# Attention 0 of a two-layer trunk: rotation stores, strip, key and query loads at other steps, weight pairs one further ahead, the last row's root taken alone

## The chip, the cores and the metric

The kernel runs on one core of a Trainium2 chip. It uses TensorE (PE, matmuls and transposes), VectorE (DVE), ScalarE (ACT), GpSimd (POOL) and SyncE (SP), which issues nearly all DMAs. The metric is the device time of one execution in microseconds. Three runs of the kernel before took 1458.23, 1456.97 and 1454.82 us, median 1456.97; the profiled execution took 1457.22 us.

## The reference

A two-layer encoder trunk on one sequence of 1024 tokens, width 1024, all in f32. Layer 0 is differential attention, layer 1 latent attention (MLA); each has a root-mean-square norm, an adaLN shift, scale and gate from a conditioning vector, a gate path, an output projection and a residual. Cut to layer 0 and the step into layer 1:

```python
h = rmsnorm(x, norm_g) * (1 + scale) + shift          # mod = silu(c) @ ada_w + ada_b
q, k, v, z = split(h @ w_in, 4)                       # 1024 columns each
q, k = rope(q), rope(k)                               # 8 heads x 2 parts x 64
for each head:                                        # v: 128 columns a head
    p0, p1 = softmax(q0 @ k0.T / 8), softmax(q1 @ k1.T / 8)
    o = (p0 - lam * p1) @ v
o = rmsnorm(o, subln_g) * (1 - lambda_init) * silu(z)
x = x + gate * (o @ w_out)
h = rmsnorm(x, norm_g1) * (1 + scale1) + shift1       # input of layer 1
```

## The kernel before, in words

**Precision.** f32 matmuls are made of three reduced ones (`mm3`, lines 178 to 180): each operand is split into a high part (a copy to the reduced format, on ACT) and a low part (a subtraction, on POOL or DVE). For weights that is `split_raw`: `wh` by ACT (L223), `wl` by POOL (L224), from a raw half strip `wraw` or `zraw` in SBUF.

**Stages**, by time of the profiled execution: norm and first projections to about 115 us; from 115 to 170 the z0 products (`z0_pair`), which make keys and queries of heads 2, 4 and 6 with seven products instead of eight and so need weight combinations as well; the value tiles to 245 us, with the first head's scores; attention 0 from 245 to 730; output projection 0 to 800; the norm into layer 1 (`group0`, rows in two groups of four 128-token tiles `xf[0..7]`) to 840; layer-1 projections to 1020; attention 1 to 1380; output projection 1 and the final norm.

**Attention 0** goes head by head. A head has eight steps, one for each tile of 128 queries: score matmuls (L1131) of `ks` against `qa` and `qb` (high and low), softmax on DVE and ACT giving `e`, transposes `tr` (L433), their high and low parts `pth` (ACT) and `ptl` (DVE), and value products `pv` on `vt`. Between these TensorE takes matmuls of `stream0`, the projection of the heads still to come: `gen_strips0` goes through `ORDER0`, the (kind, head) strips of keys, queries and gates. A strip has 16 stream steps `u`, eight for each token half, and two raw half strips; a half strip is split at u = 5 or 13 of the strip before. A head takes 32 stream steps.

**The side queue.** Small jobs wait in `side`; each stream step and each query step calls `tick`, which takes one entry off (None is a tick in which nothing is done). A projected half of keys or queries goes through `rot_job`: `fetch` (DMAs that bring rows swapped by 32 partitions), `first_`, `second` (POOL multiplications and addition), `high` (ACT's copy to the reduced format, `rp_sw`), `low` (POOL's subtraction, `rp_raw`) with the stores of both to DRAM (`hS`, L403). Keys and queries of heads 2, 4 and 6 come from the z0 products earlier; they lie in DRAM (`rS`) and are *parked*: each finished gate half (`z_done`) takes one of them into the side queue.

**Loads of a head.** `bring(h, i)` is called after step i of head h: at i = 0 it loads this head's second query half, at 4 the next head's keys (`load_k`, six DMAs), at 7 the next head's first query half (`load_q`, four DMAs, L838). Values (`vt`, L424) are loaded when a head's first value product is written. The POOL multiplications `ob` prepare output weights; `bc_d`, `bc_s` (L458, L460) broadcast a head's row norms through DRAM.

**What sets the order.** Every engine runs its instructions in a fixed order, SP's DMAs included: a DMA whose data is not ready holds what stands behind it. The order comes from the program above as a scheduling pass arranges it by its own costs; POOL's operations in the attention are held in program order (`in_turn`), ACT's copies behind the last softmax step (`behind`). So a load at another step can also move matmuls on PE.

Of the kernel before, what the change touches and what calls it, by code (L numbers as in the profile page):

```python
# [12 lines left out]
F32R = mybir.dt.float32r  # L13
# [22 lines left out]
    VEC[_n] = (NVEC, _c)  # L36
    NVEC += _c
DEF = 7
ROT = 3
FILL0 = ((1, 1, 1, 1, 1, 0), (1, 0, 1, 0, 1, 0)) * 4  # L40
FILL6 = ((1, 1, 1, 1, 0, 0), (1, 0, 1, 0, 1, 0)) * 2 + ((1, 1, 1, 0, 1, 0), (1, 0, 1, 0, 0, 0)) * 2
FILL1 = ((1, 0, 1, 0), (0, 1, 0, 0)) * 4
# [42 lines left out]
def trunk(ctx: ExitStack, tc: tile.TileContext, A, out):  # L85
# [283 lines left out]
    def rot_job(kind, h, half, eng, raw=None):  # L369

        cs = slice(half * HF, half * HF + HF)
        b = {"raw": raw}
        turn_ = in_turn if eng is G else lambda ins: ins

        def rpt(name):
            return wp.tile([P, HF], F32, name=name, tag="rp", bufs=6)

        def fetch():
            src = b["raw"]
            if src is None:  # L380
                src = rS[kind][h][half]
                b["raw"] = rpt("rp_raw")
                SP.dma_start(b["raw"], src)
            b["sw"] = rpt("rp_sw")
            for q in range(4):
                SP.dma_start(b["sw"][q * 32 : q * 32 + 32], src[(q ^ 1) * 32 : (q ^ 1) * 32 + 32])

        def first_():
            b["r"] = rpt("rp_r")
            turn_(eng.tensor_mul(b["r"], b["raw"], cosT[:, cs]))  # L390

        def second():
            turn_(eng.tensor_mul(b["sw"], b["sw"], sinT[:, cs]))
            turn_(eng.tensor_add(b["r"], b["r"], b["sw"]))

        def high():
            with behind("S"):
                S.copy(b["sw"].bitcast(F32R), b["r"])

        def low():  # L400
            turn_(eng.tensor_sub(b["raw"].bitcast(F32R), b["r"], b["sw"]))
            for l_, t in enumerate((b["sw"], b["raw"])):
                SP.dma_start(hS[kind][h][half][l_], t)  # L403

        return fetch, first_, second, high, low

    def slots(kind, h, half):
        return hS[kind][h][half].rearrange("l (c p) d -> p (l c) d", c=2)
# [404 lines left out]
    def rot_done(kind, h):  # L813
        def f(acc, half):
            raw = wp.tile([P, HF], F32, name="rp_raw", tag="rp", bufs=6)
            if kind:
                S.copy(raw, acc)
            else:
                S.mul(raw, acc, SC0)
            fetch, *steps = rot_job(kind, h, half, G, raw)  # L820
            fetch()
            side.add(*[None] * ROT, *steps[:2], None, *steps[2:])
        return f

    def load_k(h):
# [15 lines left out]
    def z_done(h):  # L841
        def f(acc, half):
            t = wp.tile([P, HF], F32, name="zth", tag="rp", bufs=6)
            S.activation(t, acc, AF.Tanh, scale=0.5)
            V.scalar_tensor_tensor(out=t, in0=t, scalar=1.0, in1=acc, op0=ALU.add, op1=ALU.mult)
            SP.dma_start(zS[h, half], t)
            if parked:
                fetch, *steps = rot_job(*parked.pop(0), G)
                side.add(fetch, None, None, *steps[:2], None, *steps[2:])
        return f  # L850

    def load_gate(h, half):
# [4 lines left out]
    def raw_of(kind, h, f):  # L857
        raw = wst.tile([P, HF], F32, name="wraw", tag="wraw", bufs=2)
        SP.dma_start(raw, A["w_s0"][kind, h, f])
        return raw  # L860

    def gen_strips0(ready, raws):

        w = ready
        for i, (kind, h) in enumerate(ORDER0):
            consume = (z_done if kind == 2 else lambda h: rot_done(kind, h))(h)
            nxt = ([], [])
            u = 0
            for half in range(2):
                for _ in gen_half(w, h0, half, lambda acc: consume(acc, half)):  # L870
                    if i + 1 < len(ORDER0) and u in (5, 13):
                        for a, b in zip(nxt, split_raw(raws.pop(0), 4)):
                            a += b
                    if i + 2 < len(ORDER0) and u in (8, 15):
                        raws.append(raw_of(*ORDER0[i + 2], u > 8))
                    u += 1
                    yield
            w = nxt
# [99 lines left out]
    def z0_weights():  # L978

        for _ in FRONT:  # L980
            a11, a12, a21, a22 = zraw[:4]
            del zraw[:4]
            w = split_raw(a11, 4)
            s1, s4 = zrt("zs1"), zrt("zs4")
            V.tensor_add(s1, a21, a22)
            V.tensor_sub(a21, a11, a21)
            V.tensor_sub(a11, s1, a11)
            V.tensor_sub(s4, a12, a11)
            yield w
            for t in (a12, s4, a11, s1, a21, a22):  # L990
                yield split_raw(t, 4)

    def product0(rhs):

# [78 lines left out]
    for half in range(2):  # L1073
        for _ in gen_half(wz0, h0, half, lambda acc: z_done(0)(acc, half)):
            side.tick()
    zq.append(next(zw))

    def late(p, i):
        if p + 1 < len(FRONT):
# [347 lines left out]
        gate_step0()  # L1427

    def bring(h, i):
        if h and i == 0:  # L1430
            load_q(h, 1)
        if h < NH - 1 and i == 4:
            load_k(h + 1)
        if h < NH - 1 and i == 7:
            load_q(h + 1, 0)

    for h in range(NH - 1):
# [260 lines left out]
    def add0(tt, acc, f, final=False):  # L1698
        V.tensor_add(xf[tt][:, halves[f]], xf[tt][:, halves[f]], acc)
        if final:  # L1700
            SP.dma_start(x1S[tt][:, halves[f]], xf[tt][:, halves[f]])
            junk = p3.tile([P, HF], BF16, name="tjunk", tag="tjunk", bufs=1)
            S.activation(junk, xf[tt][:, halves[f]], AF.Square, accum_out=(ssa, ssb)[f][tt // 4][:, tt % 4 : tt % 4 + 1])

    def group0(gi):
        fulls = [[x_] for x_ in xf[4 * gi : 4 * gi + 4]]
        V.tensor_add(ssa[gi], ssa[gi], ssb[gi])
        norm_x(ssa[gi], fulls, (2, 3) if gi else (1, 2, 3))

        def chunk(k):  # L1710
            if gi == 1:
                h1[k][1] = xt2k("h1h"), xt2k("h1l")
                h1f[k] = ut(f"h1f{k}", dt=F32)
            else:
                h1[k][0] = [h1p.tile([P, HF], F32R, name="h1_" + x_, tag="h1", bufs=16) for x_ in "hl"]
            lm["V"] = h_chunk(1, fulls, k, h1[k][gi], p3x, V, act=not gi and k in (0, 2), f32=h1f[k] if gi else None)
            if gi == 0:
                lm["h"] = h_chunk.act
                if k in (0, 4):
                    lm["h0"] = h_chunk.act  # L1720

        if gi == 0:
            side.add(*[None] * G_WAIT)
        side.add(*[lambda k=k: chunk(k) for k in ((0, 4, 1, 5, 2, 6, 3, 7) if gi else range(KT))])

    def step(sp, i):
        for _ in range((3, 3, 2, 0)[i]):
# [53 lines left out]
    for n, rows, acc, f in ((3, 4, Z, 1), (4, 0, Z, 1), (5, 4, Y, 1), (6, 4, Y, 0)):  # L1781
# [5 lines left out]
        for i in range(4):  # L1787
# [6 lines left out]
                    side.tick()  # L1794
            for j in (i,) if n < 6 or i > 1 else range(2) if i else ():
                add0(rows + j, acc[j], f, n > 3)
            if n == 4:
                SP.dma_start(x1S[i][:, halves[0]], xf[i][:, halves[0]])
                junk = p3.tile([P, HF], BF16, name="tjunk", tag="tjunk", bufs=1)
                S.activation(junk, xf[i][:, halves[0]], AF.Square, accum_out=ssa[0][:, i : i + 1])  # L1800
# [900 lines left out]
```

## Time and profile before

| | us |
|---|---|
| median of three runs | 1456.97 |
| profiled execution, its span | 1457.22, 1455.3 |
| PE, DVE, ACT, POOL busy | 1386.1, 1001.3, 734.0, 709.3 |
| share of the ending chain: PE, DVE, DMA, POOL | 65%, 11%, 7%, 6% |
| z0 products, 115 to 170: PE busy of 55 | 48.62 |
| attention 0, 245 to 730: PE busy of 485 | 445.66 |
| norm into layer 1, 800 to 840: PE busy of 40 | 36.66 |

Rows of the table by stage give the window, then busy time and instructions (x) of PE, its weight loads, DVE, ACT and POOL, then the granted PE clock (1 is full speed), the DMA share and GB/s. Rows of waits give engine and line, what ended the wait, and us in total, times, longest. Rows of the timeline give start, duration, engine, line, operation, output and inputs, and in brackets the idle time before and what ended it. A line is that of the kernel before; lines of the changed kernel stand a little higher.

### The profile page before, as it was taken

The page shows a single profiled execution, that of the slowest core. Times are in us where ns is not written, and L with a number is a line of the kernel's source. Part 1 is how long each engine was busy: PE and PEld are TensorE (multiplying, and loading weights), DVE is VectorE, ACT ScalarE, POOL GpSimd, SP SyncE. Part 2 cuts the span into 40 slices and gives each one's busy share as a digit, 9 for nine tenths or more (in the row PEclk, how much of TensorE's full clock was granted, in tenths as well). Part 3 has the DMA queues.
Part 4 walks back from the last instruction along what each step waited for, and adds up shares of the span by engine and source line. Part 5 has one row for each costly group of instructions (what it writes and reads, how often), then busy time and mean ns, then how long its engine had stood idle before and what let it go on. Part 6 is the DMA issues. An engine that isn't in the chain of part 4 may idle for free.

```text
span 1455.3 us, 20936 instructions
## 1 busy us (share of the span) xinstructions
PE 1386.1 (95%) x7298; PEld 1147.5 (79%) x7298; DVE 1001.3 (69%) x1408; ACT 734.0 (50%) x1331; POOL 709.3 (49%) x553
## 2 busy tenths in 40 slices
PE   9998899899899989999899999999999999999997
PEld 6786687788777767878788788887888888888886
DVE  7699726898678565868869796753655655455584
ACT  5533413555556454656755754334554454445554
POOL 5425730554577563734578423443023174653773
PEclk9999999999999989999999999999999999999999
DMA  9855788677668675676675415669644346565473
GB/s 344 278 163 187 231 219 247 195 217 203 195 194 244 180 222 159 211 197 194 218 245 176 143 52 164 206 216 266 200 117 131 101 124 213 179 229 172 145 269 116
DMA packets 176779, 282.41 MB, mean 194 GB/s; under 512 B 23457, under 2 KB 60449, under 8 KB 176674
## 3 DMA queue, kind: packets, MB, share of 16 engines
q1 hardware_dynamic: 176674, 281.08, 62.5%
q8 instruction: 57, 0.93, 0.3%
q14 instruction: 48, 0.39, 0.1%
HBM read 182.49 MB, written 86.98 MB: 185 GB/s over the span
## 4 chain that ended last, share of the span: by engine, by line
PE 65%; DVE 11%; DMA 7%; POOL 6%; issue 6%; ACT 4%; SPq 1%; POOLq 0%; ACTq 0%; DVEq 0%
PE s L2315 10%; PE tr L433 6%; PE acc L180 5%; PE acc L178 5%; PE acc L179 5%; PE s L1131 4%; PE pv L178 3%; PE pv L179 3%; PE pv L180 3%; PE zacc L180 2%; PE zacc L178 2%; PE zacc L179 2%; DMA qa<-hS 2%; PE vps L178 1%; PE oy L179 1%
## 5 line engine op out<-in xcount | busy, mean ns | idle before, releaser
L436 DVE TENSOR_TENSOR ptl<-tr,pth 128x512 fp32r<-128x512 f32 x256 | 175.9, 687 | 157.1 <-ACT pth L435 151.8
L435 ACT CAST pth<-tr 128x512 fp32r<-128x512 f32 x256 | 150.4, 587 | 254.6 <-PE tr L433 245.7
L450 DVE TENSOR_REDUCE nm<-s 128x1 f32<-128x1024 f32 x192 | 233.1, 1216 | 39.5 <-PE s L1131 30.6
L224 POOL TENSOR_TENSOR wl<-wraw,wh 128x512 fp32r<-128x512 f32 (+2 forms) x65 | 90.5, 1393 | 263.4 <-ACT wh L223 225.9
L452 ACT ACTIVATE e<-s,nm 128x1024 f32<-128x1024 f32 x128 | 143.3, 1120 | 98.4 <-DVE nm L450 92.6
L433 PE MATMUL tr<-ident,e 128*128 128x128 f32 x1024 | 157.5, 276 | 6.6 <-DVE ptl L436 5.9
L433 PEld LDWEIGHTS tr<-ident,e 128*128 128x128 f32 x1024 | 121.0, 142 | 51.4 <-DVE ptl L436 29.5
L178 PE MATMUL pv<-pth,vt 128*128 128x256 f32 x512 | 148.9, 291 | 1.4 <-DMA vt<-vS 1.4
L179 PE MATMUL pv<-ptl,vt 128*128 128x256 f32 x512 | 147.9, 289 | 0.0
L180 PE MATMUL pv<-pth,vt 128*128 128x256 f32 x512 | 145.3, 284 | 0.0
L180 PE MATMUL acc<-h0h,wl 128*128 128x512 f32 x264 | 109.1, 414 | 9.6 <-POOL wl L224 9.6
L178 PE MATMUL acc<-h0h,wh 128*128 128x512 f32 x264 | 109.4, 415 | 4.8 <-ACT wh L223 4.3
L1131 PE MATMUL s<-ks,qa 128*128 128x512 f32 x256 | 89.4, 431 | 21.3 <-DVE e L1139 7.8
L179 PE MATMUL acc<-h0l,wh 128*128 128x512 f32 x264 | 107.0, 405 | 0.0
L178 PEld LDWEIGHTS pv<-pth,vt 128*128 128x128 f32 x512 | 98.4, 192 | 5.4 <-DMA vt<-vS 2.2
L179 PEld LDWEIGHTS pv<-ptl,vt 128*128 128x128 f32 x512 | 98.5, 192 | 2.0
L180 PEld LDWEIGHTS pv<-pth,vt 128*128 128x128 f32 x512 | 98.4, 192 | 0.8
L1475 POOL TENSOR_TENSOR wol<-wol,woh 128x512 fp32r<-128x512 f32 x56 | 82.4, 1493 | 25.5 <-ACT woh L1474 23.8
L1131 PE MATMUL s<-ks,qb 128*128 128x512 f32 x256 | 83.5, 405 | 1.6 <-DMA qb<-hS 1.6
L1139 DVE SCALAR_TENSOR_TENSOR e<-s,z,e 128x1024 f32<-128x1024 f32 x64 | 82.1, 1284 | 2.0
L224 POOL TENSOR_TENSOR wl<-zraw,wh 128x512 fp32r<-128x512 f32 (+2 forms) x36 | 50.7, 1414 | 62.4 <-ACT wh L223 41.7
L452 ACT ACTIVATE s<-s,nm 128x1024 f32<-128x1024 f32 x64 | 70.1, 1095 | 7.1 <-DVE nm L450 6.9
(470 smaller groups left out, 3595.0 us busy)
## 6 DMA issues: line engine op xcount, KB each, us to landing
ada<-in_ada_ss SPq DMA_DIRECT2D x32, 512.0 KB, 5.6
vt<-vS SPq DMA_DIRECT2D x32, 512.0 KB, 5.5
wol<-tS SPq DMA_DIRECT2D x56, 256.0 KB, 5.1
wraw<-in_w_s SPq DMA_DIRECT2D x52, 256.0 KB, 3.2
vS<-v_hl SPq DMA_DIRECT2D x24, 512.0 KB, 5.9
tS<-ob SPq DMA_DIRECT2D x48, 256.0 KB, 3.9
bc_s<-bc_d SPq DMA_DIRECT2D x34, 256.0 KB, 4.0
gz<-zS SPq DMA_DIRECT2D x32, 256.0 KB, 4.2
```

What stands on the lines that cost most here:

```text
L178: PE.matmul(psum, ah, bh, start=first, stop=False, skip_group_check=skip)
L179: PE.matmul(psum, ah, bl, start=False, stop=False, skip_group_check=skip)
L180: mm3.last = PE.matmul(psum, al, bh, start=False, stop=last, skip_group_check=skip).ins
L224: sub = (V if pair_of else G).tensor_sub(l_[:, :n], raw[:, :n], f32v(h_[:, :n]))
L433: transpose_p.last = PE.transpose(tr[:, j, :], p[:, kt * P : (kt + 1) * P], ident).ins
L435: mk["S"] = S.copy(pth[kh][:, :, dst], tr).ins
L436: mk["V"] = V.tensor_sub(ptl[kh][:, :, dst], tr, f32v(pth[kh][:, :, dst])).ins
L450: mk["V"] = V.reduce_max(nm, s_ps, axis=AX.X, negate=True).ins
L452: mk["S"] = S.activation(e, s_ps, AF.Exp, bias=nm, scale=1.0, accum_out=zs).ins
L1131: PE.matmul(s_ps[:, kc * HF : (kc + 1) * HF], src[:, c, ql], KS[h][kc][:, c, :], start=fst, stop=not fst)
L1475: sub = eng.tensor_sub(lo, raw, f32v(hi))
L2315: PE.matmul(s_ps[:, kc * HF : (kc + 1) * HF], lhs, rhs(kc), start=i == 0, stop=i == 4)
```

## The change

1. **Stores.** The store of a rotated tile is a step of its own (`store`), not part of `low`. For stream halves two ticks (ROT) pass ahead of `first_`, not three; `high` and `low` come two ticks sooner, and the store comes two ticks behind `low`, in the tick where it stood before. For parked halves `high` and `low` come one tick sooner, the store one later.
2. **Strip loads.** A raw half strip is loaded at u = 12 (first half) of the strip two before, or u = 3 (second half) of the strip before, not at u = 8 and 15 of the strip two before.
3. **Keys and queries.** `bring` loads the next head's keys at i = 2 (was 4), its first query half at i = 5 or 6 (was 7), and the second half of odd heads at i = 1 (was 0).
4. **Weight pairs.** Two pairs of z0 weights are split ahead of the first product (was one), so `product0` runs two ahead; every fourth pair goes into buffers of the tag `gz`, which the gates of heads use later (`split_z`).
5. **Last row.** In `group0(1)` the sum and root of rows 4 to 6 are taken as soon as row 6 is complete (`root1(0, 3)`), that of row 7 alone behind them; rows 4 and 5 are scaled on ACT, row 6 on DVE, the halves of row 7 on DVE and ACT.

```diff
--- before.py
+++ after.py
@@ -36,7 +36,7 @@
     VEC[_n] = (NVEC, _c)
     NVEC += _c
 DEF = 7
-ROT = 3
+ROT = 2
 FILL0 = ((1, 1, 1, 1, 1, 0), (1, 0, 1, 0, 1, 0)) * 4
 FILL6 = ((1, 1, 1, 1, 0, 0), (1, 0, 1, 0, 1, 0)) * 2 + ((1, 1, 1, 0, 1, 0), (1, 0, 1, 0, 0, 0)) * 2
 FILL1 = ((1, 0, 1, 0), (0, 1, 0, 0)) * 4
@@ -399,10 +399,12 @@
 
         def low():
             turn_(eng.tensor_sub(b["raw"].bitcast(F32R), b["r"], b["sw"]))
+
+        def store():
             for l_, t in enumerate((b["sw"], b["raw"])):
                 SP.dma_start(hS[kind][h][half][l_], t)
 
-        return fetch, first_, second, high, low
+        return fetch, first_, second, high, low, store
 
     def slots(kind, h, half):
         return hS[kind][h][half].rearrange("l (c p) d -> p (l c) d", c=2)
@@ -819,7 +821,7 @@
                 S.mul(raw, acc, SC0)
             fetch, *steps = rot_job(kind, h, half, G, raw)
             fetch()
-            side.add(*[None] * ROT, *steps[:2], None, *steps[2:])
+            side.add(*[None] * ROT, *steps[:2], None, *steps[2:4], None, steps[4])
         return f
 
     def load_k(h):
@@ -846,7 +848,7 @@
             SP.dma_start(zS[h, half], t)
             if parked:
                 fetch, *steps = rot_job(*parked.pop(0), G)
-                side.add(fetch, None, None, *steps[:2], None, *steps[2:])
+                side.add(fetch, None, None, *steps[:2], None, *steps[2:4], None, steps[4])
         return f
 
     def load_gate(h, half):
@@ -871,8 +873,10 @@
                     if i + 1 < len(ORDER0) and u in (5, 13):
                         for a, b in zip(nxt, split_raw(raws.pop(0), 4)):
                             a += b
-                    if i + 2 < len(ORDER0) and u in (8, 15):
-                        raws.append(raw_of(*ORDER0[i + 2], u > 8))
+                    if i and i + 1 < len(ORDER0) and u == 3:
+                        raws.append(raw_of(*ORDER0[i + 1], 1))
+                    if i + 2 < len(ORDER0) and u == 12:
+                        raws.append(raw_of(*ORDER0[i + 2], 0))
                     u += 1
                     yield
             w = nxt
@@ -980,7 +984,7 @@
         for _ in FRONT:
             a11, a12, a21, a22 = zraw[:4]
             del zraw[:4]
-            w = split_raw(a11, 4)
+            w = split_z(a11)
             s1, s4 = zrt("zs1"), zrt("zs4")
             V.tensor_add(s1, a21, a22)
             V.tensor_sub(a21, a11, a21)
@@ -988,7 +992,18 @@
             V.tensor_sub(s4, a12, a11)
             yield w
             for t in (a12, s4, a11, s1, a21, a22):
-                yield split_raw(t, 4)
+                yield split_z(t)
+
+    zn = [0]
+
+    def split_z(raw):
+        zn[0] += 1
+        if zn[0] % 4:
+            return split_raw(raw, 4)
+        h_, l_ = [wst.tile([P, HF], F32R, name="zw" + x_, tag="gz", bufs=3) for x_ in "hl"]
+        S.copy(h_, raw)
+        in_turn(G.tensor_sub(l_, raw, f32v(h_)))
+        return [[t[:, k * P : (k + 1) * P] for k in range(4)] for t in (h_, l_)]
 
     def product0(rhs):
 
@@ -1073,7 +1088,7 @@
     for half in range(2):
         for _ in gen_half(wz0, h0, half, lambda acc: z_done(0)(acc, half)):
             side.tick()
-    zq.append(next(zw))
+    zq += [next(zw), next(zw)]
 
     def late(p, i):
         if p + 1 < len(FRONT):
@@ -1427,11 +1442,11 @@
         gate_step0()
 
     def bring(h, i):
-        if h and i == 0:
+        if h and i == h % 2:
             load_q(h, 1)
-        if h < NH - 1 and i == 4:
+        if h < NH - 1 and i == 2:
             load_k(h + 1)
-        if h < NH - 1 and i == 7:
+        if h < NH - 1 and i == 5 + (h + 1) % 2:
             load_q(h + 1, 0)
 
     for h in range(NH - 1):
@@ -1700,12 +1715,15 @@
         if final:
             SP.dma_start(x1S[tt][:, halves[f]], xf[tt][:, halves[f]])
             junk = p3.tile([P, HF], BF16, name="tjunk", tag="tjunk", bufs=1)
-            S.activation(junk, xf[tt][:, halves[f]], AF.Square, accum_out=(ssa, ssb)[f][tt // 4][:, tt % 4 : tt % 4 + 1])
+            add0.sq = S.activation(junk, xf[tt][:, halves[f]], AF.Square, accum_out=(ssa, ssb)[f][tt // 4][:, tt % 4 : tt % 4 + 1]).ins
 
     def group0(gi):
         fulls = [[x_] for x_ in xf[4 * gi : 4 * gi + 4]]
-        V.tensor_add(ssa[gi], ssa[gi], ssb[gi])
-        norm_x(ssa[gi], fulls, (2, 3) if gi else (1, 2, 3))
+        if gi:
+            last_row()
+        else:
+            V.tensor_add(ssa[gi], ssa[gi], ssb[gi])
+            norm_x(ssa[gi], fulls, (1, 2, 3))
 
         def chunk(k):
             if gi == 1:
@@ -1722,6 +1740,25 @@
         if gi == 0:
             side.add(*[None] * G_WAIT)
         side.add(*[lambda k=k: chunk(k) for k in ((0, 4, 1, 5, 2, 6, 3, 7) if gi else range(KT))])
+
+    y1 = []
+
+    def root1(a, b):
+        V.tensor_add(ssa[1][:, a:b], ssa[1][:, a:b], ssb[1][:, a:b])
+        w = ssa[1][:, a:b]
+        lm["w"] = V.tensor_scalar(w, w, 1.0 / D, EPS, op0=ALU.mult, op1=ALU.add).ins
+        return rsqrt(w, b - a)
+
+    def last_row():
+        (y,) = y1
+        yl = root1(3, 4)
+        with tc.issue_after(add0.sq):
+            for j in range(2):
+                S.mul(xf[4 + j], xf[4 + j], y[:, j : j + 1])
+        with tc.issue_after(lm["w"]):
+            V.tensor_scalar(xf[6], xf[6], y[:, 2:3], None, op0=ALU.mult)
+        V.tensor_scalar(xf[7][:, halves[1]], xf[7][:, halves[1]], yl[:, 0:1], None, op0=ALU.mult)
+        lm["h"] = S.mul(xf[7][:, halves[0]], xf[7][:, halves[0]], yl[:, 0:1]).ins
 
     def step(sp, i):
         for _ in range((3, 3, 2, 0)[i]):
@@ -1794,6 +1831,8 @@
                     side.tick()
             for j in (i,) if n < 6 or i > 1 else range(2) if i else ():
                 add0(rows + j, acc[j], f, n > 3)
+            if n == 6 and i == 2:
+                y1.append(root1(0, 3))
             if n == 4:
                 SP.dma_start(x1S[i][:, halves[0]], xf[i][:, halves[0]])
                 junk = p3.tile([P, HF], BF16, name="tjunk", tag="tjunk", bufs=1)
```

Three places of the new order. First SP's queue at the first query half of head 5 (`hS_131`; `hS_132` is its second half), before:

```order
L846 DMA zS<-zth 128x512
L458 DMA bc_d<-rq_y 128x4
L1174 DMA oF_81<-o 128x512
L1364 DMA tS_83<-ob_4897 128x512
L1364 DMA tS_83<-ob_4898 128x512
L460 DMA bc_s<-bc_d 128x512
L859 DMA wraw<-in_w_s 128x512
L838 DMA qa<-hS_131 64x2x512 x2
L838 DMA qb<-hS_131 64x2x512 x2
```

and now:

```order
L848 DMA zS<-zth 128x512
L405 DMA hS_132<-rp_raw 128x512
L1189 DMA oF_81<-o 128x512
L840 DMA qa<-hS_131 64x2x512
L460 DMA bc_d<-rq_y 128x4
L840 DMA qa<-hS_131 64x2x512
L840 DMA qb<-hS_131 64x2x512
L462 DMA bc_s<-bc_d 128x512
L840 DMA qb<-hS_131 64x2x512
```

The query loads moved from behind the broadcast `bc_s` and a strip load to directly behind the store of `o`; one of the four still stands behind the broadcast.

Second POOL around the low half of the strip that TensorE needs at about 386 us, before:

```order
L401 TENSOR_TENSOR rp_raw<-rp_r,rp_sw 128x512
L1215 TENSOR_TENSOR rq_y<-rq_y,sl_f 128x4
L390 TENSOR_TENSOR rp_r<-rp_raw,cosT 128x512
L393 TENSOR_TENSOR rp_sw<-rp_sw,sinT 128x512
L394 TENSOR_TENSOR rp_r<-rp_r,rp_sw 128x512
L224 TENSOR_TENSOR wl<-wraw,wh 128x512
```

and now:

```order
L401 TENSOR_TENSOR rp_raw<-rp_r,rp_sw 128x512
L174 TENSOR_TENSOR rq_y<-sl_w,mhalf 128x4
L1230 TENSOR_TENSOR rq_y<-rq_y,sl_f 128x4
L390 TENSOR_TENSOR rp_r<-rp_raw,cosT 128x512
L224 TENSOR_TENSOR wl<-wraw,wh 128x512
L393 TENSOR_TENSOR rp_sw<-rp_sw,sinT 128x512
L394 TENSOR_TENSOR rp_r<-rp_r,rp_sw 128x512
```

The low half now stands ahead of the last two rotation operations. At the strip of about 519 us it moved likewise from behind two scalings of `ob` to ahead of them.

Third the first value product of head 2 on PE (`h0h_0_186` and so on are the projection's operands, in the order of its steps), before:

```order
L178 MATMUL acc<-h0h_0_186,wh 128x512
L179 MATMUL acc<-h0l_0_187,wh 128x512
L180 MATMUL acc<-h0h_0_186,wl 128x512
L178 MATMUL acc<-h0h_0_190,wh 128x512
L179 MATMUL acc<-h0l_0_191,wh 128x512
L180 MATMUL acc<-h0h_0_190,wl 128x512
L1131 MATMUL s<-ks,qa 128x512 x2
L1131 MATMUL s<-ks,qb 128x512
L178 MATMUL pv<-pth,vt 128x256
```

and now:

```order
L178 MATMUL acc<-h0h_0_202,wh 128x512
L179 MATMUL acc<-h0l_0_203,wh 128x512
L180 MATMUL acc<-h0h_0_202,wl 128x512
L178 MATMUL acc<-h0h_0_206,wh 128x512
L179 MATMUL acc<-h0l_0_207,wh 128x512
L180 MATMUL acc<-h0h_0_206,wl 128x512
L1146 MATMUL s<-ks,qa 128x512 x2
L1146 MATMUL s<-ks,qb 128x512 x2
L178 MATMUL pv<-pth,vt 128x256
```

The product moved four projection groups (190 to 206) of three matmuls further back. On SP, the six key loads of head 3 now stand ahead of the two value loads of head 2, where they stood behind them; it is so for heads 0 to 6.

## The prediction

> **What bounds the kernel now.** I read the page first (busy shares and slices), then the table by stage, then TensorE's waits within the stages that the change touches, and from each large wait back to its cause.
>
> ```profile
> PE 1386.1 (95%) x7298; PEld 1147.5 (79%) x7298; DVE 1001.3 (69%) x1408; ACT 734.0 (50%) x1331; POOL 709.3 (49%) x553
> 115.00:170.00 55.00, 48.62 (x207) 38.11 (x206) 44.52 (x60) 22.39 (x41) 31.67 (x23) 1.00 0.64 214
> 245.00:730.00 485.00, 445.66 (x2470) 367.24 (x2469) 367.39 (x529) 271.56 (x483) 267.10 (x221) 0.97 0.70 203
> 1020.00:1380.00 360.00, 359.19 (x2188) 307.97 (x2187) 204.42 (x285) 186.46 (x340) 155.74 (x123) 1.00 0.51 159
> ```
>
> TensorE is busy 1386.1 of 1455.3 us, so 69 us is all that any change of order could take out. It lies unevenly: attention 1 (1020 to 1380) idles 0.8 us and cannot give anything, attention 0 (245 to 730) idles 485.0 − 445.7 = 39.3 us, the z0 products (115 to 170) 6.4. The granted clock is 0.97 in attention 0, 1.00 in the other two. So the question is which waits make up the 39.3, and which of them the change addresses. TensorE's waits of 245 to 730, by the instruction that ended them:
>
> ```profile
> PE s L1131 <- DVE e L1139: 7.5, 11, 1.7
> PE s L1131 <- DMA qa<-hS: 7.2, 4, 3.4
> PE s L1131 <- ACT e L452: 6.0, 5, 2.2
> PE acc L180 <- POOL wl L224: 5.8, 6, 2.3
> PE tr L433 <- DVE ptl L436: 4.1, 7, 1.1
> PE acc L178 <- ACT wh L223: 3.9, 6, 0.9
> PE s L1131 <- DMA qb<-hS: 1.6, 1, 1.6
> PE pv L178 <- DMA vt<-vS: 1.4, 2, 0.7
> ```
>
> These add up to 37.5 us. The softmax chain (e from DVE and ACT, ptl) has 17.6 of it and is not edited. Query loads have 8.8, the low halves of weight strips on GpSimd 5.8, value loads 1.4.
>
> **Queries.** The two long waits on queries open heads 5 and 6. First the scores that wait, each the first row of its head, then windows right behind long stalls (us, TensorE's busy time, granted clock, DMA share, GB/s):
>
> ```profile
> 566.72 1.77 PE L1131 MATMUL s<-ks,qa 128*128 128x512 f32 x4 [2.98 <-DMA qa<-hS]
> ...
> 627.87 1.53 PE L1131 MATMUL s<-ks,qa 128*128 128x512 f32 x4 [3.42 <-DMA qa<-hS]
> ```
>
> ```profile
> 567.00:570.40 3.40, 3.40 (x11) 0.50 1.06 309
> 628.50:631.90 3.40, 3.40 (x12) 0.50 1.08 234
> 386.10:389.50 3.40, 3.23 (x8) 0.50 0.74 190
> 519.20:522.60 3.40, 3.40 (x9) 0.51 0.46 115
> 361.00:364.40 3.40, 3.32 (x20) 1.00 0.80 216
> ```
>
> SyncE issued head 5's queries from 558.96 on, behind a broadcast that waits for its own write, and behind a strip load. In the new order the first of these loads stands ahead of both, right behind the store of o that was issued at 554.88:
>
> ```profile
> 554.88 0.44 SPq L1174 DMA_DIRECT2D oF<-o  x1
> ...
> 558.96 1.26 SPq L838 DMA_DIRECT2D qa<-hS  x2
> ```
>
> That is up to 4.1 us sooner against a wait of 2.98. The call also moves from step 7 of a head to step 5 or 6: a head takes 627.87 − 566.72 = 61.15 us for eight steps, 7.6 each, so 7.6 to 15 us are offered. The data (rotated queries) are written by stores that SyncE reaches sooner too, below. I take the two long waits (6.4) and the one on qb (1.6) as gone, the two small ones (0.8) as left: **−8.0**; the bounds are 0 (something else on the queue holds them) and −8.8.
>
> **What follows a long stall.** Behind the stall at 566.72 stands a window of 3.40 us in which TensorE is fully busy at a granted clock of 0.50; behind the 1.6 us wait on qb (at 361) the clock stays 1.00. A busy engine at half clock loses 1.7 us in such a window. Two windows belong to the query stalls (567.0 and 628.5) and two to strip stalls (386.1 and 519.2), so 4 × 1.7 = **−6.8** if all four stalls shrink below two microseconds, 0 if none does. The Trainium skill, "TensorE: Matmul & The Clock Gate" (Why this matters for your kernels), warns of idle gaps over about 3 us, one idle window returning the array to half clock. By it only the two query stalls would buy clock back, −3.4 and not −6.8; the row at 386.10 disagrees, since its gap was 2.29 us.
>
> **Strips.** Low halves are made on GpSimd in program order. The two long waits:
>
> ```profile
> 386.27 0.79 PE L180 MATMUL acc<-h0h,wl 128*128 128x512 f32 x1 [2.29 <-POOL wl L224]
> ...
> 519.09 0.69 PE L180 MATMUL acc<-h0h,wl 128*128 128x512 f32 x1 [2.00 <-POOL wl L224]
> ```
>
> and what GpSimd did just ahead of them, with the row of the raws' landing:
>
> ```profile
> 382.36 1.30 POOL L393 TENSOR_TENSOR rp_sw<-rp_sw,sinT 128x512 f32<-128x512 f32 x1
> 383.74 1.27 POOL L394 TENSOR_TENSOR rp_r<-rp_r,rp_sw 128x512 f32<-128x512 f32 x1
> ...
> 515.31 2.51 POOL L1374 TENSOR_TENSOR ob<-ob,c 128x512 f32<-128x512 f32 x2
> ...
> wraw<-in_w_s SPq DMA_DIRECT2D x52, 256.0 KB, 3.2
> ```
>
> The new order puts the first of these strips ahead of the two rotation operations (2.57 us against 2.29) and the second ahead of two scalings of the output weights (2.51 against 2.00), so 4.3 of the 5.8 should go: **−4.3**, bounds 0 and −5.8. Moving the strip's load four stream steps later costs nothing as long as it lands before the split: the last row gives 3.2 us to landing, and the new places lie nine and ten steps ahead of their splits; with 32 steps in a head of 61.15 us that is 17 us. If that cover went, each late half strip could cost up to one landing.
>
> **Stores.** The store of a rotated tile was issued in the tick that queued the last subtraction; SyncE then stood there:
>
> ```profile
> SPq L403 <- ACT rp_sw L398: 77.2, 21, 8.5
> ...
> SPq L403 <- POOL rp_raw L401: 26.3, 20, 5.8
> ```
>
> 103 us of queue time, during which everything behind it (queries, values, keys, strips) waited too. With two ticks between, most of it leaves the queue. I cost this at nothing of its own: its gain is what lets the query loads start, counted above.
>
> **Keys against values.** Keys come two steps sooner, and now stand directly ahead of values:
>
> ```profile
> 390.62 0.39 PE L180 MATMUL acc<-h0h,wl 128*128 128x512 f32 x1
> 390.84 0.39 PE L178 MATMUL acc<-h0h,wh 128*128 128x512 f32 x1
> ...
> 393.01 0.38 PE L178 MATMUL pv<-pth,vt 128*128 128x256 f32 x1 [0.62 <-DMA vt<-vS]
> ```
>
> ```profile
> 535.40 0.63 SPq L829 DMA_DIRECT2D ks<-hS  x1
> ...
> 538.01 1.24 SPq L831 DMA_DIRECT2D ks<-hS  x2
> ```
>
> Values had no slack at head 2 (the third row waits 0.62). Head 5's six key loads take 539.25 − 535.40 = 3.85 us of SyncE's queue. Against that, TensorE's new order has the first value product later: at head 2 by four projection groups more, 12 matmuls at 0.22 us (390.62 to 390.84) = 2.6 us, besides further rows ahead of them. I take **+2.0** for all heads, bounds −1.4 (today's waits gone) and 7 × 3.85 = +27.0 (all seven heads that load a next one).
>
> **Weight pairs ahead.** In the z0 products and the value tiles behind them the waits are:
>
> ```profile
> PE acc L180 <- POOL wl L224: 3.8, 2, 2.2
> PE zacc L180 <- POOL wl L224: 3.3, 4, 1.1
> PE zacc L178 <- DVE zth L845: 2.8, 1, 2.8
> PE zacc L178 <- ACT wh L223: 1.0, 1, 1.0
> ```
>
> One more pair of weights is ready ahead of each product, which reaches the 3.3 and 1.0; the extra pairs use three buffers that the gates of head 0 held, whose loads move to just before their use. The 3.8 is the first stream strip, whose splits now stand further forward among the value weights' subtractions on GpSimd. DVE's 2.8 stays. I take half of 8.1 plus half of one half-clock window (177.9): **−4.9**; bounds 0 (GpSimd is the limit: 31.67 busy of 55, so not by load) and −9.8.
>
> **Last row.** TensorE waits 2.8 us for the scaled rows:
>
> ```profile
> PE trh L522 <- DVE x L511: 2.8, 1, 2.8
> 825.59 2.41 DVE L511 TENSOR_SCALAR x<-x,rq_y 128x1024 f32<-128x1024 f32 x2 [1.12 <-POOL rq_y L174]
> ```
>
> The root now has three rows early and one alone, and behind the last root stand two half rows on two engines instead of two full rows each: 2.41 falls to about a quarter, 0.6. **−1.8**; the bounds are −2.8 and +0.5 (an extra root and two small DVE operations in the chain).
>
> **Sum.** Attention and z0 take −8.0 − 6.8 − 4.3 − 4.9 = −24.0. A TensorE that arrives sooner meets the softmax chain, or DVE in z0 (44.5 busy of 55), as its next limit. By the first list that chain ends 17.6 of 37.5, 47%, so I give 47% back: +11.3. With −1.8 and +2.0: −24.0 + 11.3 − 1.8 + 2.0 = −12.5. The profiled execution took 1457.22 (span 1455.3 and 1.9 around it), 0.25 above the median 1456.97. 1457.2 − 12.5 = 1444.7, say **1444.5**, own range 1436 to 1451.
>
> **Rivals.**
> *Values late (slower).* One mechanism: the value load stands behind the six key loads and lands after TensorE gets there. For it: no slack at head 2. Against: the later first product. It decides where queue plus landing exceed that move, more than about 4 us. Four heads at 3.85 plus a half-clock window each, 15.4 + 6.8 = 22.2, on top of −14.5 without my +2.0: 1457.2 − 14.5 + 22.2 = 1465. The Trainium skill, "DMA: Bandwidth & Descriptors" (Queues, rings and completion order), speaks for it: each DMA engine takes one issuer's descriptors in ring order, so values issued behind keys also queue behind their bytes; no row here separates that from the issue time.
> *Softmax takes all.* DVE is busy 367 of 485 us in attention 0 and e ends more waits than anything. If every removed wait returns as one on e or ptl, only −1.8 + 2.0 and a little of z0 remain: 1455, between 1452 and 1459. Against it: the query stalls are at head starts, where no older score is in work.
> *Queries not sooner.* If the rotation chain (ACT's cast, GpSimd's subtraction) and not SyncE's queue is late, the store waits stay and −8.0 and their two windows of −3.4 fall away, of which 53% was counted: +6.0, 1450.5.
>
> **Numbers.** Forecast 0.45, queries not sooner 0.15, softmax takes all 0.22, values late 0.16, under 1433 0.02. A change below 0.2% (2.9 us) cannot be told from none here. Faster: 0.45 + 0.15 + 0.02 + 0.05 of softmax = 0.67; same 0.14; slower 0.16 + 0.03 = 0.19. The range 1433 to 1460 leaves out most of the slow rival and a little below.
>
> **What would show it.** Right: the waits on qa and qb in attention 0 under 1.5 us together, wl under 2, SyncE's wait on rp_sw under 30, no 0.50 window at heads 5 and 6, trh's wait about 1. Wrong: a vt wait over 4 us, waits on e and ptl grown from 17.6 to 30, or qa waits that stay behind an unchanged rp_sw wait.

## The result, and the profile after

The changed kernel takes 1442.72 us (median of four runs, 1441.84 to 1443.20) where the kernel before took 1455.89 in the same comparison: ratio 0.9907, 95% interval 0.989 to 0.9924, by that ratio 13.6 us less, with 11 to 16 in the interval. The forecast was 1444.5 us, with a sum of −12.5. The profiled execution has a span of 1440.7 us against 1455.3.

The table by stage of the changed kernel (columns as before: window, busy us of PE, its weight loads, DVE, ACT, POOL, granted PE clock, DMA share, GB/s):

```profile
115.00:170.00 55.00, 51.21 (x213) 41.63 (x214) 43.17 (x58) 21.18 (x39) 29.21 (x20) 0.94 0.60 199
245.00:720.00 475.00, 441.52 (x2484) 362.83 (x2482) 372.81 (x531) 274.09 (x485) 268.79 (x223) 0.99 0.69 208
```

Attention 0 idles 475.0 − 441.5 = 33.5 us where it idled 39.3, and its granted clock is 0.99 where it was 0.97. In the z0 products the clock fell, 1.00 to 0.94. TensorE's waits in attention 0 now:

```profile
PE tr L435 <- DVE ptl L438: 8.1, 16, 0.9
PE s L1146 <- DVE e L1154: 7.5, 11, 2.1
PE s L1146 <- ACT e L454: 4.1, 6, 1.5
PE acc L180 <- POOL wl L224: 3.8, 4, 1.9
PE s L1146 <- DMA qa<-hS: 3.5, 2, 2.6
PE pv L178 <- DMA vt<-vS: 1.6, 2, 1.2
PE pv L178 <- ACT pth L437: 1.4, 2, 0.7
PE acc L178 <- ACT wh L223: 1.3, 3, 0.7
PE s L1146 <- DMA qb<-hS: 1.0, 1, 1.0
```

These nine are 32.3 us, the eight of before were 37.5. Queries fell from 8.8 to 4.5, strips (wl, wh) from 9.7 to 5.1; ptl doubled from 4.1 to 8.1. SyncE's own waits on the stores hardly moved:

```profile
SPq L405 <- ACT rp_sw L398: 61.0, 16, 11.3
SPq L405 <- POOL rp_raw L401: 39.2, 19, 6.2
```

The windows at half clock in attention 0 and, for contrast, the same stretch behind the starts of heads 5 and 6:

```profile
420.75:424.15 3.40, 3.10 (x8) 0.52 1.06 321
454.75:461.55 6.80, 6.34 (x14) 0.52 1.04 371
536.35:539.75 3.40, 3.06 (x15) 0.59 0.00 0
555.60:559.00 3.40, 3.36 (x18) 1.00 0.81 250
613.30:616.70 3.40, 3.40 (x19) 1.00 0.98 227
```

Added up over the stage in such windows, 13.6 us of attention 0 run near half clock (the first three rows) where it was 30.6 before (nine times 3.4 us; the four that the prediction shows are among them). The first score of head 3 still waits for its queries, and a half-clock window lies there; head 5 waits less, and head 6 is not among the waits any more:

```profile
421.05 1.19 PE L1146 MATMUL s<-ks,qa 128*128 128x512 f32 x2 [2.55 <-DMA qa<-hS]
...
555.64 0.73 PE L1146 MATMUL s<-ks,qa 128*128 128x512 f32 x2 [0.90 <-DMA qa<-hS]
```

The score matmuls on qa, first and last start, in the kernel before and in the changed one:

```profile
L1131 PE MATMUL s<-ks,qa x256: 387/396/796, 220.9 to 731.3; 128*128 128x512 f32 x128
```

```profile
L1146 PE MATMUL s<-ks,qa x256: 387/396/764, 219.8 to 718.2; 128*128 128x512 f32 x128
```

So of the 14.6 us between the two spans 1.1 came before attention 0, 12.0 within it, 1.5 behind it.

### The profile page after: what moved, and what is told of

Its sections match the earlier page's. It is cut to its first block, busy times and chain, and to the rows that moved or that the text cites. A ratio compares the mean times of both kernels' runs of the same rounds, so it can differ in the third digit from the quotient of the medians.

```text
span 1440.7 us, 20945 instructions
## 1 busy us (share of the span) xinstructions
PE 1380.8 (96%) x7298; PEld 1143.4 (79%) x7298; DVE 1003.4 (70%) x1410; ACT 735.5 (51%) x1332; POOL 719.7 (50%) x554
## 4 chain that ended last, share of the span: by engine, by line
PE 69%; DVE 10%; DMA 6%; POOL 5%; ACT 4%; issue 4%; SPq 1%; POOLq 0%; ACTq 0%; DVEq 0%
PE s L2354 10%; PE tr L435 6%; PE acc L180 6%; PE acc L178 6%; PE acc L179 6%; PE s L1146 5%; PE pv L178 3%; PE pv L179 3%; PE pv L180 3%; PE zacc L178 2%; PE zacc L180 2%; PE zacc L179 2%; DVE nm L452 2%; DVE ada L476 2%; PE vps L178 1%
## 5 line engine op out<-in xcount | busy, mean ns | idle before, releaser
L452 DVE TENSOR_REDUCE nm<-s 128x1 f32<-128x1024 f32 x192 | 233.2, 1216 | 26.6 <-PE s L1146 17.5
L1490 POOL TENSOR_TENSOR wol<-wol,woh 128x512 fp32r<-128x512 f32 x56 | 81.8, 1483 | 26.8 <-ACT woh L1489 24.3
L1146 PEld LDWEIGHTS s<-ks,qa 128*128 128x128 f32 x256 | 42.9, 192 | 30.1 <-ACT e L454 7.9
```

Source lines behind the costliest of these rows:

```text
L452: mk["V"] = V.reduce_max(nm, s_ps, axis=AX.X, negate=True).ins
L1146: PE.matmul(s_ps[:, kc * HF : (kc + 1) * HF], src[:, c, ql], KS[h][kc][:, c, :], start=fst, stop=not fst)
```

## The experiments

Runs of one kernel spread more on the chips of the experiments than on the first (the kernel before from 1451 to 1465), so each result is the ratio to the kernel before, run beside it, with its interval; (ratio − 1) × 1457 gives us. The changed kernel and the pieces of its loads stand in one table at the end of this section.

**No load moved.** Everything as changed but `bring`:

```diff
-        if h and i == h % 2:
+        if h and i == 0:
             load_q(h, 1)
-        if h < NH - 1 and i == 2:
+        if h < NH - 1 and i == 4:
             load_k(h + 1)
-        if h < NH - 1 and i == 5 + (h + 1) % 2:
+        if h < NH - 1 and i == 7:
             load_q(h + 1, 0)
```

> The changed kernel with key and query loads back at their old steps (i = 4, 7, 0); everything else as changed. Theory (query stalls and the half-clock windows behind them were the largest piece): the waits on qa and qb return to about 8.8 us, the half-clock windows at heads 5 and 6 return, and the time is 5 to 8 us above the changed kernel, about 1449. Rival 1 (the stores, which free the queue, carry the gain, and the loads' place does not matter): within 2 us of the changed kernel, about 1443, with the qa wait still under 5. Rival 2 (the gain is in the reordered matmuls: this piece alone moves over 2000 rows on TensorE, the others a few hundred): the waits on e, ptl, wl and vt change as much as those on qa.

Measured: 0.997 (0.9957 to 0.9982), 4.4 us under before; so 9 to 10 of the 14 us go with the moved loads. But the waits on queries did not return as my theory had it. Waits of this kernel in attention 0, and windows behind some of its stalls (TensorE alone):

```profile
PE s L1146 <- DVE e L1154: 9.3, 10, 2.0
PE s L1146 <- ACT e L454: 6.0, 6, 1.6
PE acc L180 <- POOL wl L224: 5.8, 8, 2.0
...
PE s L1146 <- DMA qb<-hS: 2.6, 2, 1.4
```

```profile
455.60:462.40 6.80, 5.76 (x16) 0.52 0.98 336
503.20:506.60 3.40, 2.95 (x7) 0.56 0.58 178
520.20:523.60 3.40, 3.40 (x9) 0.57 0.64 165
530.40:533.80 3.40, 2.66 (x11) 0.58 0.46 118
```

Long waits on qa are not in the list; wl is as long as before and e of DVE longer (9.3 against 7.5), and the time at half clock is 27.2 us, these four rows and 10.2 us in two more stretches. Against the changed kernel's 13.6 that is up to 6.8 us of time, over half of the 11.9 that separate the two profiles; against the 20.4 of a second profile of the changed kernel it would be 3.4. The second rival, that the matmuls' order matters (this piece moves over 2000 rows on TensorE), was open from here.

**Stores in one step with the last subtraction again** (ROT 3, `store` back in `low`).

```diff
-ROT = 2
+ROT = 3
...
         def low():
             turn_(eng.tensor_sub(b["raw"].bitcast(F32R), b["r"], b["sw"]))
-
-        def store():
             for l_, t in enumerate((b["sw"], b["raw"])):
                 SP.dma_start(hS[kind][h][half][l_], t)
...
-            side.add(*[None] * ROT, *steps[:2], None, *steps[2:4], None, steps[4])
+            side.add(*[None] * ROT, *steps[:2], None, *steps[2:])
```

> The changed kernel with the stores again in the same step as the last subtraction (ROT 3). Theory of the prediction (the stores held SyncE's queue, and so the queries): SyncE's wait on rp_sw grows from 61 back to about 77 us, the qa wait grows from 3.5 to about 6, the time is 2 to 4 us above the changed kernel, 1445 to 1447. Rival (the queue's wait was hidden by the earlier call of the loads alone): within 1.5 us of the changed kernel, whatever rp_sw does.

Measured: 0.9922 (0.9898 to 0.9946). SyncE's waits and TensorE's on queries:

```profile
SPq L403 <- ACT rp_sw L398: 73.0, 20, 10.8
SPq L403 <- POOL rp_raw L401: 34.8, 20, 6.2
```

```profile
PE s L1144 <- DMA qa<-hS: 5.8, 2, 3.2
```

The store waits grow from 100 to 108 us only, the waits on qa from 3.5 to 5.8 (a second profile of the changed kernel has 5.0). The time is 2.6 us above the changed kernel, inside both intervals: as expected by size, but not resolved.

**One weight pair ahead, no pairs in the gate buffers.**

```diff
-            w = split_z(a11)
+            w = split_raw(a11, 4)
...
-                yield split_z(t)
+                yield split_raw(t, 4)
...
-    zq += [next(zw), next(zw)]
+    zq.append(next(zw))
```

> The changed kernel with one weight pair ahead and no pairs in the gate buffers. From the two traces the first score comes at 220.9 us before and at 219.8 after, so theory: this piece is worth about 1.1 us, the time 1443.5 to 1444. Rival (the prediction's 2.6 net, the trace's 1.1 being spoiled by a half-clock window of 6.8 us that fell behind the DVE wait at 118 us by chance): the first score comes 2 to 3 us later without it.

Measured: 0.9894 (0.9866 to 0.9922): no slower without this piece. Neither the 1.1 nor the 2.6 us is visible in the whole, and the first score comes at 220.2 us, where two profiles of the changed kernel have 219.8 and 221.1.

**The old norm of the last four row tiles.**

```diff
-        if gi:
-            last_row()
-        else:
-            V.tensor_add(ssa[gi], ssa[gi], ssb[gi])
-            norm_x(ssa[gi], fulls, (1, 2, 3))
+        V.tensor_add(ssa[gi], ssa[gi], ssb[gi])
+        norm_x(ssa[gi], fulls, (2, 3) if gi else (1, 2, 3))
...
-            if n == 6 and i == 2:
-                y1.append(root1(0, 3))
```

> The changed kernel with the old norm of the last four row tiles. This piece moves rows on no engine outside the stage from about 780 to 830 us. Theory: the wait on DVE's scaled rows returns (2.8 against 1.0 now), the time is 1.4 to 1.8 us above the changed kernel. Rival (the stall only moves to the next stage's first sums): within 0.5 us.

Measured: 0.9918 (0.9891 to 0.9944), 2 us above the changed kernel, not resolved; the wait returned in full:

```profile
PE trh L524 <- DVE x L513: 2.9, 1, 2.9
```

**Only the keys, only the queries, and the three loads alone.** Of the block of the first experiment, one kernel moves only `load_k` to i = 2, one only the first query half to 5 or 6; a third is the kernel before with nothing but all three loads moved.

> The changed kernel with only the key loads moved (i = 2), first queries at 7 and second at 0 as before. Without any load moved the waits on queries were already down to 3.2 us and the time stayed 9 us above the changed kernel, so the query stalls cannot be the gain. Theory now (order): earlier key loads stand ahead of the value loads, and so the scheduler places value products later on TensorE; the new order of matmuls has fewer long stalls and half-clock windows behind them. Then the keys alone, which move 2599 rows on TensorE, bring most of the 9 us: 1445 to 1448. Rival (queries after all): the keys alone stay at 1452 to 1455.

> The changed kernel with only the first query loads moved (i = 5 or 6), keys at 4 and second queries at 0 as before. Order theory: 1386 rows move on TensorE from head 2 on, part of the gain, 1449 to 1453, and the waits that fall are not those on queries. Rival (queries): nearly the changed kernel, 1443 to 1446, with qa and qb under 1 us.

> The kernel before with nothing but the three loads moved; stores, strips, weight pairs and last row as before. Order theory: 2860 rows move on TensorE without the other pieces, and most of the 9 us come: 1448 to 1451 where the kernel before has 1458. Rival (the loads need the queue that the stores free): within 3 us of before, qa waits of 6 us or more.

> The changed kernel itself, on the chip of the other pieces. All theories: 0.9907 of the kernel before, about 1444.5 where before is 1458. If the half-clock windows fall by chance, its runs spread by 3 to 5 us as those of the pieces did.

Measured: keys 1.0092 (1.0068 to 1.0116), queries 0.9922 (0.9893 to 0.995), the loads alone 0.9926 (0.9897 to 0.9955), the changed kernel 0.9904 (0.9873 to 0.9935). The order theory's expectation was wrong by its sign: the keys alone, which it gave the gain, make the kernel slower than before, and the queries alone bring what all loads bring, as far as the intervals tell. The loads alone, with the stores as before, bring 10.8 us, so the rival by which they need the queue that the stores free fell as well. The waits of that kernel in attention 0:

```profile
PE s L1131 <- DMA qb<-hS: 4.1, 2, 2.8
...
PE s L1131 <- DMA qa<-hS: 3.7, 1, 3.7
...
PE acc L180 <- POOL wl L224: 2.5, 4, 0.7
```

It still waits 7.8 us on queries, where the kernel before waits 8.8, and the kernel with no load moved waits 3.1 and is slower: in the scheduler's order the waits on queries and the time do not go together. It has 20.5 us at half clock, where the kernel before has 30.6.

With early keys and late queries, heads start with long waits; head 4's first score and SyncE's issue of its queries:

```profile
502.77 2.05 PE L1146 MATMUL s<-ks,qa 128*128 128x512 f32 x4 [6.36 <-issue]
```

```profile
492.45 1.33 SPq L840 DMA_DIRECT2D qa<-hS  x2
```

"Issue" means that no releaser was recorded; the second of these two loads landed 9.5 us behind its issue at 493.2, at 502.7, just ahead of the score. But both theories were still mixed, since every one of these pieces also rearranges TensorE.

**A fixed order.** TensorE's instructions of heads 0 to 6 are held in program order, so that in the four kernels DVE, POOL and TensorE have the same order, row for row, wherever the loads stand (six rows of ACT differ where the keys move):

```diff
+    class Pinned:
+        def matmul(self, *a, **k):
+            ins = nc.tensor.matmul(*a, **k)
+            return tc.keep_in_program_order(ins) if pin[0] else ins
...
+    PE = Pinned()
...
+    pin[0] = True
     for h in range(NH - 1):
         attn0(h, ...)
+    pin[0] = False
```

> Stores, strips, weight pairs and last row as changed, loads at their old steps, and TensorE's instructions of heads 0 to 6 held in the order of the program, so that moving a load can no longer move a matmul. This and the next three have the same order on TensorE, DVE and GpSimd, row for row; only SyncE differs (and six rows on ScalarE). Order theory (moving loads helps or hurts because the matmuls are rearranged): all four lie within 2 us of each other. Load theory (what counts is when the data lands): this one has the waits on qa and qb, 5 to 9 us of them, and lies 5 us or more above the one with all loads moved. The level itself is open, 1440 to 1465.

> The same fixed order, only the key loads moved to i = 2. Order theory: within 2 us of the one without moved loads; the 16 us that the keys alone cost were the matmuls' order. Load theory: the six key loads ahead of the values and queries hold these up, 5 us or more slower than without, with waits on vt or on qa.

> The same fixed order, only the first query loads moved to i = 5 or 6. Order theory: within 2 us. Load theory: 5 us or more faster than without, the waits on qa and qb gone.

> The same fixed order, all loads of the change moved. Order theory: within 2 us of the others. Load theory: as the queries alone, plus what the keys cost in the queue. If the fixed order is as good as the scheduler's, this is at or below the changed kernel, 1440 to 1445.

Measured, with the scheduler's order beside it (us against the kernel before, half the interval behind ±):

| loads moved | scheduler's order | fixed order |
|---|---|---|
| none | −4.4 ± 1.8 | −4.8 ± 2.3 (0.9967) |
| queries | −11.4 ± 4.1 | −10.8 ± 2.0 (0.9926) |
| keys | +13.4 ± 3.5 | +9.6 ± 1.9 (1.0066) |
| all | −14.0 ± 4.5 | +9.3 ± 1.8 (1.0064) |

"Queries" moves the first query halves alone; "all" moves the second halves of odd heads too. In a fixed order the loads' landing decides, and it decides both ways. Queries: −6.0 ± 3. The kernel with no load moved, its wait and the clock behind it, then the same stretch with queries moved:

```profile
PE pv L92 <- DMA vt<-vS: 9.4, 2, 4.8
...
PE s L92 <- DMA qb<-hS: 4.5, 2, 3.5
```

```profile
553.35:560.15 6.80, 5.74 (x16) 0.51 1.07 269
```

```profile
554.50:561.30 6.80, 6.80 (x36) 1.00 0.99 267
```

The 4.5 us of wait and this window are gone, and values wait 2.2 us more (11.6 in the other kernel). In these two executions that is all: each has 23.9 us at half clock in the stage, since the other kernel has longer windows elsewhere, and their spans (1447.3 and 1444.9) differ by 2.4, about 4.5 − 2.2. What makes up the rest of the −6.0 of all runs is not shown.

Keys: +14.4 alone, +20.1 (with the second query halves) on top of the queries. With all loads moved, the wait on values, then SyncE and TensorE around head 3's second value half:

```profile
PE pv L92 <- DMA vt<-vS: 26.6, 4, 7.5
```

```profile
446.63 0.58 SPq L843 DMA_DIRECT2D ks<-hS  x1
...
460.13 1.08 SPq L845 DMA_DIRECT2D ks<-hS  x2
...
462.36 0.43 SPq L438 DMA_DIRECT2D vt<-vS  x1
```

```profile
468.28 0.55 PE L92 MATMUL pv<-pth,vt 128*128 128x256 f32 x1 [7.55 <-DMA vt<-vS]
```

Key loads begin at 446.63 and the value load stands behind the last of them, at 462.36; of the 15.7 us between, the key loads themselves take 3.3, and the rest is stores, fetches, broadcasts and other loads that stand among them, with what they wait for. The landing of the value ends the wait at 468.28. TensorE waits 7.55 us, and the clock is low around the stall:

```profile
462.40:472.60 10.20, 4.32 (x16) 0.52 1.03 332
```

Against the kernel with only the queries moved, the waits on values grow by 15.0 us (26.6 against 11.6), and TensorE's busy time at half clock in the stage from 15.8 to 24.3, half of which is 4.2: together 19.2, where the two spans differ by 17.9.

In the scheduler's order the keys stand ahead of the values too, but the value products stand later, and vt costs 1.6 us. The difference between the columns in the last row, 14.0 + 9.3 = 23.3 us, is what the scheduler's rearrangement (of TensorE and, with it, of SyncE's queue) is worth when all loads move; in the other three rows the two orders are equal within their intervals.

## Why the prediction was right, point by point

The total was right, with a sum in which two sizes, the gross 24.0 and the 11.3 given back, were both too large; that they cancelled is luck. Of the 12.0 us within attention 0 the listed waits account for 37.5 − 32.3 = 5.2, and time at half clock for up to (30.6 − 13.6) / 2 = 8.5, less where TensorE stood idle in such a window. The two together are more than the 12.0, and it is an account of two single executions, not of the medians.

*Queries, −8.0 with −3.4 of clock, at 53% −6.0.* Right, as far as the fixed order shows it: there moving them is worth −6.0 ± 3. In the changed kernel heads 5 and 6 lost their long waits (0.90 and none are left) and their windows. What I said would show it, under 1.5 us left, did not hold: 4.5 remain, 2.55 of it at head 3. The chain that ended there has the obstacle named in the prediction, a broadcast ahead on SyncE's queue, and behind it a landing of 6.38 us:

```profile
412.27 1.84 DMA bc_d<-rq_y
...
414.53 6.38 DMA qa<-hS
...
421.05 2.04 PE s L1146 x4
```

*The clock, −6.8.* Right in kind, in size by chance: the four named windows went, others came, and the net is up to 8.5. A second profile of the changed kernel has 20.4 us at half clock in attention 0 where this one has 13.6, which would make it 5.1. The prediction's bound of 69 us, TensorE's idle time, left this out: a matmul at half clock counts as busy, and TensorE's busy time fell from 1386.1 to 1380.8 us.

*Strips, −4.3.* Half in size, and not by the cause given. wl fell from 5.8 to 3.8, wh from 3.9 to 1.3; both long waits went from their places, and another strip is late now (1.89 us at 527.86, behind a rotation that waited for ACT). But the kernel with the strip loads moved and no other load has 5.8 on wl, as before, and the one with only keys and queries moved, its strip loads at their old steps, has 2.5 (rows above). So the fall goes with the order that the moved loads bring, and nothing shows a gain of the strip piece.

*Stores, nothing of their own, "most of it leaves the queue".* Wrong. rp_sw and rp_raw held SyncE 103 us and hold it 100. SyncE still comes to the store ahead of ACT's copy, 16 times where it was 21, and the longest wait grew from 8.5 to 11.3; why two ticks between changed so little is not shown. So the condition of the third rival, that the store waits stay, was met, and its price was not: the loads called at earlier steps gained without the queue, 10.8 us in the kernel that has the loads alone. The whole of stores, strips, pairs and last row is worth 4.4 us; which of them has how much the runs don't resolve.

*Keys against values, +2.0, and the rival at +22.2.* Near, and each in its own order. In the scheduler's order vt costs 1.6 us, 0.2 more than before (2.5 in the second profile). With the matmuls held, the same key loads cost 14.4 to 20.1 us, with 26.6 us of waiting on values at four heads, close to the rival's sum, though where the delay is shown most of it is not the keys' own 3.3 us of queue but what the scheduler put among them; with the matmuls rearranged they cost nothing that can be measured. What the rival had against itself, the later value products, fits both; that no other part of the rearrangement has a share in it is not shown. That keys alone are slower than before in the scheduler's order too (+13.4) I had not foreseen: there the next head's queries are what is late.

*Weight pairs, −4.9, net −2.6.* Too much. TensorE's waits between 112 and 245 us now:

```profile
PE zacc L178 <- DVE zth L847: 4.4, 1, 4.4
PE acc L180 <- POOL wl L224: 4.0, 1, 4.0
```

The pairs' own waits (3.3 and 1.0) are gone as reckoned. But the wait on DVE that I let stand grew from 2.8 to 4.4, and the clock of this stage fell to 0.94; the first strip's two waits (3.8) became one of 4.0, since its second half stands behind four subtractions of value weights in a row:

```profile
167.18 5.99 POOL L1074 TENSOR_TENSOR tk<-wvr,tk 128x512 fp32r<-128x512 f32 x4
173.12 2.24 POOL L224 TENSOR_TENSOR wl<-wraw,wh 128x512 fp32r<-128x512 f32 x1
```

*Last row, −1.8.* Right in kind: trh waits 1.0, as said, with 0.7 and 0.3 beside it. The run without the piece has the 2.9 back, and its time differs by 2 us, which its interval doesn't settle.

*47% back to the softmax chain, +11.3.* Wrong in size. e and ptl went from 17.6 to 19.7 (17.7 in the second profile). Where the removal of a wait failed it was because the wait stayed (queries, strips, z0), not because softmax took it; a gross sum of 24 was too large by about what I gave back.

One correction to the words on the change ahead of the prediction (the diff is right): counted in ticks, `high` and `low` of a stream half come one tick sooner and its store one later; of a parked half `high` and `low` stand where they were and the store two later. The terms of the sum did not use these counts.

## What to carry to other kernels

A load that is moved on one queue is paid by what stands behind it there, and by what comes to stand between; ask in the same breath where its neighbour's consumer will stand. Where a scheduler places both, test a load's place with the consumer's order held, or two effects of 20 us can hide in a change of none. And look at the clock behind the stalls: in the two profiles compared here it was up to 8.5 us in attention 0, more than the listed waits, and up to 5.1 with the second profile of the changed kernel.

## What the runs showed of the hardware

Two things I had not expected. First, it is not the length of one stall that decides about the clock. It changes on a grid of 3.41 us (the stretches shown as 3.40, 6.80 and 10.20 us are one, two and three steps of it), and what goes with a half-clock window is how long TensorE idled in the full-clock window just ahead. In the changed kernel three stalls of 0.66, 0.68 and 0.34 us within one window were enough (TensorE alone):

```profile
533.54:536.95 3.41, 1.73 (x12) 1.00 0.52 182
536.95:540.36 3.41, 3.41 (x16) 0.50 0.01 2
```

Over the fourteen profiles of this document, attention 0 has 64 full-clock windows with more than 1.65 us of idle time, just under half a window, and 58 of them are followed by half clock; of the 1810 with less, 2 are. The stall at 361 of the kernel before, behind which the prediction saw a clock of 1.00, left 1.64 us idle in its window. This is a count over profiles; no kernel was built to test it.

The Trainium skill, "TensorE: Matmul & The Clock Gate" (What's actually happening), has a free-running window of 3413 ns by which activity is judged; the stretches here agree with that length. The advice of the same page (Why this matters for your kernels), no gaps over about 3 us, is too wide for these rows.

Second, the half-clock time near the start falls differently from one execution of a program to the next. The same four matmuls in two profiles of the changed kernel, before anything that the change touches:

```profile
4.92 1.98 PE L642 MATMUL cb<-crow,ones 1*128 1x512 f32 x4 [0.20 <-DVE crow L638]
```

```profile
5.13 3.78 PE L642 MATMUL cb<-crow,ones 1*128 1x512 f32 x4 [0.30 <-DVE crow L638]
```

They took twice as long in the second profile. From 12.40 to 17.85 us it is the other way round: the first profile has a granted clock of 0.50 there, the second 1.00. (The second profile's clock is not recorded ahead of 12.69 us and reads 1.00 there, so at its start only the durations tell.) Why the runs of one kernel differ, the kernel before from 1451 to 1465 us on the experiments' chips, was not tested; this may be a part of it.

Not tried: the fixed order with only the queries moved, freed of the one long wait that all four kernels of that order have at the start of attention 0 (8.9 us on e of ACT); it might beat the changed kernel.
